# Interleaving the second half's attention with the first half's MLP in a one-core encoder layer

## The chip, the core and the metric

The kernel runs on one core of a Trainium2 chip. The core has a matrix engine (TensorE, PE in the profile; its weight loads are PEld), three elementwise engines (VectorE or DVE, ScalarE or ACT, GpSimd or POOL), and a queue engine (SyncE or SP) from which this kernel issues all its DMAs. TensorE results land in PSUM, which has eight banks of 512 float32 columns; everything else lies in SBUF, on 128 partitions. The engines run their own instruction streams in order and wait for one another by semaphores.

The metric is the device time of one execution in microseconds (us), the median of the runs shown.

## The reference, cut to what matters

One layer of a hybrid encoder: 1024 tokens, width 1024, float32.

```
mod = silu(c) @ w_ada + b_ada                 -> sh_a, sc_a, g_a, sh_m, sc_m, g_m
h    = rmsnorm(x) * (1+sc_a) + sh_a
proj = h @ w_in   -> q_lat (256), kv_lat (128), k_rope (32), ca_qkv (3 x 8 heads x 64)
q    = rmsnorm(q_lat) @ w_q_up                -> 8 heads x 96, QK-norm, rotary on 32
k, v = rmsnorm(kv_lat) @ w_kv_up (+ k_rope)   -> 8 heads x (96, 64), QK-norm, rotary
o_mla = softmax(q k / sqrt(96), keys of own and earlier 64-token chunks) @ v
cq, ck = rmsnorm(per head of ca_qkv)
o_ca  = softmax(cq ck / 8 + relative bias, own chunk and 8 chunks to the left) @ cv
x   = x + g_a * (concat(o_mla, o_ca) @ w_out)
h   = rmsnorm(x) * (1+sc_m) + sh_m
u   = causal_depthwise_conv3(h @ w_up) + b    -> gate, val (2816 each)
x   = x + g_m * ((silu(gate) * val) @ w_down)
```

Two facts decide what can overlap. The attention is causal by chunks, so the first 512 tokens need no key of the last 512. And everything after the attention is per token, except that the convolution of a token needs the up-projection of the two tokens before it.

## The kernel before

**Precision.** Every large float32 product is three products of a reduced-precision form: each operand is split into a high part and a low rest, and `gemm3` (L144) adds high x high, high x low and low x high, at L148, L149 and L150. The split of a weight tile is an ACT copy (`hi_of`, L75) and a subtraction on POOL or DVE (`lo_of`, L82). The softmax weights and V are split into two half-precision parts instead; there the product with V is a chain of 128 x 128 matmuls (L714).

**Stages.** The layer is done for all 1024 tokens, stage after stage:

1. Start (L191 to L326): eight tiles of x are loaded and normalised; for each of eight 128-channel slices d, a 1 MB piece of `w_ada` is reduced on DVE (L239, L241) to the shift and scale, the slice of x is transposed and modulated into the pages `hT` (L219 to L228), and the first block of the input projection is accumulated (`qk0`). Then come the rotary tables (L260), a chain of small DVE instructions.
2. Attention. A unit is four query tiles of 128 tokens of one head (`Unit`, L626). `scores` (L634) makes the scores of one query tile against all its keys in PSUM (L656), the row minimum (DVE L667, L671 or L675; the signs are turned), the exponential (ACT L681), the two half-precision parts (POOL L71 and DVE L701) and a DMA transpose of them (L703). `values` (L707) multiplies with V three tiles later (`DEPTH`), and after four tiles L721 and L722 combine the parts and the result goes to DRAM (`oT_d`). All units of the chunked heads come first, in both token halves, then all units of the latent heads (L812, L813).
3. Between the tiles of the attention, fillers (L771) put other products in: the V and q/k projections (`f_v`, `f_qk`), the latent block (`f_m`), the up-projections of the latent heads (`f_up`) and the output projection of the chunked heads (`f_oca`). `pace` (L803) releases fillers in proportion to the attention's matmul time, with the factor 1.9 beside the chunked heads and 0.5 beside the latent ones. A second list, `f_ada` (L417), reduces the other rows of `w_ada` on DVE.
4. Output projection of the latent heads, residual, second norm and the pages `h2` (L834 to L879), with nothing beside them; then the MLP's gate row (L896 to L908), again alone.
5. MLP (L910 to L963). For each of 44 channel tiles, `up_tile` loads and splits a 512 KB weight tile, makes 48 matmuls of 512 columns (24 for each token half), and applies the convolution (ACT L923, DVE L924, L925). For each pair of channel tiles `ff_tile` forms silu(gate) x val, splits it, and prepares a `w_down` tile. `down` takes two such results at a time and adds them into the residual rows x1 (DVE L951).

**What sets the order.** The program gives dependences and priorities only; a scheduler at build time orders each engine's instructions by a simulated clock, and gives a tile a buffer from the free ones of its tag. `tc.high_priority` lifts the attention's steps, `issue_after` (L161) holds a filler's matmuls behind the attention's recent ones. At run time each engine then takes its instructions in that fixed order. The buffers of the attention, of the transition and of the MLP are separate pools, opened and closed one after another; PSUM likewise (psA, psB, psC).

## Time and profile before

| | us |
|---|---|
| median of 3 runs | 1525.28 (1518.91 to 1527.24) |
| span of the profiled execution | 1526.0 |
| PE busy | 1338.1 |
| DVE busy | 824.4 |
| POOL busy | 664.7 |
| ACT busy | 487.4 |

No time of the profiled execution other than its span is given; the span lies among the three measured times, 0.7 us above their median, so what lies around it is too small to be told from the spread. DMA moved 142.90 MB, at 94 GB/s on average.

In the profile a matmul's duration contains its way through the array, and neighbours overlap: the 512-column matmuls of the MLP are listed at 390 ns, yet 442 of them start in 100 us, one in 226 ns. So a busy PE may still have room, and what TensorE must do is better counted as matmuls times their spacing.

### The profile page before, as it was taken

How to read it: one execution, taken by the hardware profiler on the slowest of the kernel's cores; microseconds unless marked ns; L12 is line 12 of the kernel's file. 1: busy time of each engine (PE TensorE's matmuls, PEld its weight loads, DVE VectorE, ACT ScalarE, POOL GpSimd, SP SyncE). 2: the span in 40 equal slices, each digit the busy share in tenths (PEclk: the TensorE clock that was granted, in tenths of full speed). 3: DMA queues.
4: the chain of work that ended last, by engine and by line, in shares of the span. 5: the costliest groups of instructions: out<-in, count | busy, mean ns of one | idle time of the engine just before them, and what ended most of it. 6: DMA issues, size and time to landing. Idle time of an engine off the chain costs nothing.

```text
span 1526.0 us, 19445 instructions
## 1 busy us (share of the span) xinstructions
PE 1338.1 (88%) x7100; PEld 1111.0 (73%) x7100; DVE 824.4 (54%) x1536; ACT 487.4 (32%) x919; POOL 664.7 (44%) x720
## 2 busy tenths in 40 slices
PE   3859989998767888858739999999999999999997
PEld 2749878987646666646528888888888888888885
DVE  6864786566768768843742433344334343434343
ACT  5443353343545545532413211212122121221200
POOL 5264463473799735435725231514314142341510
PEclk9979978989878899977859999999999999999998
DMA  7323657463613678787142110202112020110202
GB/s 270 133 67 73 138 119 142 121 131 94 122 40 70 150 143 174 165 181 247 56 138 69 56 55 28 70 30 67 42 42 69 15 83 28 56 56 28 70 1 110
DMA packets 202460, 142.90 MB, mean 94 GB/s; under 512 B 146294, under 2 KB 181242, under 8 KB 201340
## 3 DMA queue, kind: packets, MB, share of 16 engines
q1 hardware_dynamic: 202364, 141.66, 36.0%
q8 instruction: 56, 0.92, 0.3%
q14 instruction: 40, 0.33, 0.1%
HBM read 93.90 MB, written 13.11 MB: 70 GB/s over the span
## 4 chain that ended last, share of the span: by engine, by line
PE 63%; DMA 14%; DVE 10%; POOL 7%; issue 3%; ACT 2%; SPq 1%; POOLq 0%; DVEq 0%; ACTq 0%
PE up L148 10%; PE up L149 10%; PE up L150 10%; DMA aw<-w_ada 6%; PE dn L148 5%; PE dn L149 5%; PE dn L150 5%; DMA PTm<-hlm 4%; PE sc L656 2%; DVE adacc L241 2%; DVE aacc L428 1%; PE sm L656 1%; PE pvc L714 1%; POOL hlm L71 1%; DMA adaw<-w_ada 1%
## 5 line engine op out<-in xcount | busy, mean ns | idle before, releaser
L148 PE MATMUL up<-hT,wu_h 128*128 128x512 f32 x704 | 275.1, 391 | 0.0
L149 PE MATMUL up<-hT,wu_h 128*128 128x512 f32 x704 | 274.3, 390 | 0.0
L150 PE MATMUL up<-hT,wu_l 128*128 128x512 f32 x704 | 274.1, 389 | 0.0
L951 DVE TENSOR_TENSOR x<-x,dn 128x1024 f32<-128x1024 f32 x88 | 107.4, 1220 | 179.8 <-PE dn L150 179.8
L924 DVE SCALAR_TENSOR_TENSOR u<-up,pk,u 128x1023 f32<-128x1023 f32 x44 | 56.4, 1283 | 232.1 <-ACT u L923 232.1
L923 ACT ACTIVATE u<-up,pk 128x1024 f32<-128x1024 f32 x44 | 53.1, 1208 | 386.0 <-PE up L150 386.0
L149 PEld LDWEIGHTS up<-hT,wu_h 128*128 128x128 f32 x704 | 132.4, 188 | 28.0 <-issue 0.5
L148 PEld LDWEIGHTS up<-hT,wu_h 128*128 128x128 f32 x704 | 132.4, 188 | 27.9 <-issue 0.5
L82 POOL TENSOR_TENSOR wu_l<-wu_r,wu_h 128x1024 fp32r<-128x1024 f32 x44 | 105.7, 2402 | 107.9 <-PE up L149 60.1
L150 PEld LDWEIGHTS up<-hT,wu_l 128*128 128x128 f32 x704 | 132.4, 188 | 27.7 <-POOL wu_l L82 0.2
L77 POOL TENSOR_SCALAR wd<-wd_r 128x1024 fp32r<-128x1024 f32 x22 | 23.1, 1050 | 290.2 <-PE dn L150 289.1
L148 PE MATMUL dn<-wd,g 128*128 128x512 f32 x352 | 138.0, 392 | 5.0 <-ACT g L75 5.0
L149 PE MATMUL dn<-wd,g 128*128 128x512 f32 x352 | 137.9, 392 | 0.0
L150 PE MATMUL dn<-wd,g 128*128 128x512 f32 x352 | 137.4, 391 | 0.0
L71 POOL TENSOR_SCALAR hlm<-Pm,rim 128x512 f16<-128x512 f32 (+4 forms) x88 | 62.8, 717 | 69.1 <-DMA PTm<-hlm 46.6
L75 ACT ACTIVATE wu_h<-wu_r 128x1024 fp32r<-128x1024 f32 x44 | 46.5, 1057 | 141.1 <-DMA wu_r<-w_up 141.1
L938 POOL TENSOR_TENSOR wd_r<-wd_r,gmbc 128x1024 f32<-128x1024 f32 x22 | 52.6, 2392 | 80.6 <-DMA wd_r<-w_down 80.6
L701 DVE SCALAR_TENSOR_TENSOR hlm<-Pm,rim,hlm 128x512 f16<-128x512 f32 (+4 forms) x88 | 70.2, 801 | 31.7 <-POOL hlm L71 31.4
L148 PEld LDWEIGHTS dn<-wd,g 128*128 128x128 f32 x352 | 66.6, 189 | 19.4 <-issue 5.4
L71 POOL TENSOR_SCALAR hlc<-Pc,ric 128x640 f16<-128x640 f32 (+2 forms) x64 | 45.9, 719 | 78.5 <-DVE ric L684 38.9
L656 PE MATMUL sm<-mk,mq 96*128 96x512 f32 (+3 forms) x288 | 70.0, 375 | 9.8 <-ACT Pm L681 9.0
L656 PE MATMUL sc<-k,q 64*128 64x512 f32 (+3 forms) x288 | 71.2, 376 | 7.4 <-ACT Pc L681 4.9
(276 smaller groups left out, 3031.8 us busy)
## 6 DMA issues: line engine op xcount, KB each, us to landing
wu_r<-w_up SPq DMA_DIRECT2D x44, 512.0 KB, 3.6
aw<-w_ada SPq DMA_DIRECT2D x96, 128.0 KB, 2.2
wd_r<-w_down SPq DMA_DIRECT2D x22, 512.0 KB, 3.5
x<-x SPq DMA_DIRECT2D x16, 512.0 KB, 9.3
adaw<-w_ada_a SPq DMA_DIRECT2D x8, 1024.0 KB, 4.8
wq_r<-w_qk SPq DMA_DIRECT2D x32, 128.0 KB, 2.6
wor<-w_out SPq DMA_DIRECT2D x16, 256.0 KB, 3.0
cl<-oT_d SPq DMA_DIRECT2D x16, 256.0 KB, 3.3
```

The source lines that it names most:

```text
L71: pool.tensor_scalar(o, i, s, 1.0, op0=MUL, op1=MUL)
L75: act.activation(o, i, AF.Copy)
L82: (pool if eng == "p" else dve).tensor_tensor(o, i, f32(hi), op=SUB)
L148: pe.matmul(pt, sh, mh, start=(start and i == 0), stop=False)
L149: pe.matmul(pt, sh, ml, start=False, stop=False)
L150: pe.matmul(pt, sl, mh, start=False, stop=(stop and i == n - 1))
L656: last = pe.matmul(s[:, c:c + w], qpg[rs_, a, q], kpgs[kh][rs_, b, ko:ko + w], start=(a == 0 and b == 0), stop=(a == 1))
L701: dve.scalar_tensor_tensor(hl[:, w:2 * w], pp, ri[:], hl[:, :w], op0=MUL, op1=SUB)
L923: act.activation(u[:], pt[:], AF.Identity, scale=pk[:, cv + 2:cv + 3], bias=pk[:, cv + 3:cv + 4])
L924: dve.scalar_tensor_tensor(u[:, 1:], pt[:, :S - 1], pk[:, cv + 1:cv + 2], u[:, 1:], op0=MUL, op1=ADD)
L938: pool.tensor_tensor(raw[:], raw[:], gmbc[:], op=MUL)
L951: dve.tensor_tensor(x1[t][:], x1[t][:], pt[:], op=ADD)
```

## The change

The layer is cut into two halves of 512 tokens, h = 0 and h = 1.

- The start does only the first half: four tiles of x, pages `hT` of half 0, and the latent block instead of the first q/k block. The reduction of the first two `w_ada` pieces moves from DVE to TensorE, as products with one moving column.
- The first attention round runs all 16 heads of half 0. Its fillers are the projections of half 0 and of half 1 (`f_up`, `f_qk`, `f_v`, each now called once for each half, and so loading and splitting its weights twice), and `f_hT1` and `f_m1` for half 1. The factor of `pace` is 3.4.
- The finished q and k pages of half 1, the k pages of half 0 and all V tiles are written to DRAM (`keep_page`, `keep_v`) and read back by the units that use them (`get_page`, `load_v`).
- The second round runs all heads of half 1. Its fillers are the MLP's gate row, the whole output projection, residual and norm of half 0 (`f_op`, all eight heads' rows at once, no partial sums in DRAM), and the MLP of half 0. The factor is 4.0.
- Last come `f_op` and the MLP of half 1. The MLP therefore loads and splits all its weights twice. Each `up_tile` has 24 matmuls and a 512-column result; the convolution's two edge columns are carried from half 0 to half 1 (`cvt`, `cvc`).
- All SBUF tiles come from one pool with a fixed number of slots for each role (`BUFS`), all PSUM tiles from another (`PB`). The result tiles of `up_tile` and `down` shrink from two buffers of 1024 columns each to two shared buffers of 512.

```diff
+    BUFS = {"H": 10, "X": 4, "w": 8, "raw": 2, "g": 3, "T": 8, "pg": 5, "HL": 3, "PT": 3, "R": 8,
+            "V": 2, "bias": 2, "tg": 1}
+    PB = {"S": 2, "mm": 2, "T": 1, "pv": 1}
...
+    def load_cols(name, src, ncol, kk, he="a", le="p", ssw=None):
...
+        for k0 in range(0, ND, kk):
+            raw = sb("raw", [P, kk, ncol], f"{name}r{k0}")
+            sp.dma_start(raw[:], src[:, k0:k0 + kk, :])
...
+            hi = sb("w", [P, kk, ncol], f"{name}h{k0}", F32R)
+            lo = sb("w", [P, kk, ncol], f"{name}l{k0}", F32R)
+            hi_of(he, hi[:], raw[:])
+            lo_of(le, lo[:], raw[:], hi[:])
...
+    for d in range(ND):
+        if d + 2 < ND:
+            load_ada(d + 2)
+        pt = psum("mm", f"p_ada{d}")
+        for i in range(2):
+            for k in range(ND):
+                pe.matmul(pt[:, i:i + 1], wada[d, i][:, k], cs[:, k:k + 1], start=(k == 0), stop=(k == ND - 1))
...
+        hT[d, 0] = mod_transpose(lambda j: xs[j][:, d * P:(d + 1) * P], d, 0, 0, ("T", "pv")[d % 2],
+                                 "H", "a", "v" if d % 2 else "p")
...
+    def keep_page(key, pg, rows):
+        d = dram.tile([P, 2, 512], F32, name="pgd_" + "_".join(map(str, key)))
+        sp.dma_start(d[:rows], f32(pg[:rows]))
+        pg_d[key] = d
+
+    def get_page(key, rows):
+        pg = sb("pg", [P, 2, 512], "pgl_" + "_".join(map(str, key)), F32R)
+        sp.dma_start(f32(pg[:rows]), pg_d[key][:rows])
+        return pg
...
+    def f_qk(p, h):
+        w = load_cols(f"wq{p}{h}_", I["w_qk"][p], 256, 4)
+        qn = sb("T", [P, 4, 256], f"qn{p}_{h}")
...
+        if h == 0:
+            qns[p] = qn
+        else:
+            for kind, c, gain in (("q", 0, None), ("k", P, gk_ca[:])):
+                pg = qk_page(lambda j: qn[:, j, c:c + P], f"{kind}{p}_1", P, gain)
+                keep_page(("c", p, kind, 1), pg, P)
+                yield 440
...
+        def load_v(u, grp, hd):
+            u.v = sb("V", [P, 8, P], f"vl{u.nm}_{u.g}", F16)
+            for h in range(u.g + 1):
+                sp.dma_start(u.v[:, 4 * h:4 * h + 4], v_d[grp, h][:, :, hd])
...
-                if n <= 640:
-                    pr = at.tile([P, 640], F32, name=f"P{nm}", tag="P", bufs=P_BUFS)
-                else:
-                    pr = pgtile([P, 1024], F32, f"P{nm}")
+                pr = sb("R", [P, 512], f"P{nm}") if n <= 512 else sb("T", [P, 1024], f"P{nm}")
...
+            else:
+                u.pages = (get_page(("m", gr, hh, "q", 1), QK), [get_page(("m", gr, hh, "k", i), QK) for i in range(2)])
...
+    def f_op(h, otag, xtag, ntag, h2tags):
+        oh = []
+        for t in range(4):
+            x1[h, t] = sb(xtag, [P, D], f"x1_{h}{t}")
+            sp.dma_start(x1[h, t][:], I["x"][(4 * h + t) * P:(4 * h + t + 1) * P, :])
+            lo = sb(otag, [P, ND, P], f"ol{h}{t}", F32R)
+            hi = sb(otag, [P, ND, P], f"oh{h}{t}", F32R)
+            for k in range(ND):
+                sp.dma_start(f32(lo[:, k]), oT_d[h][k][:, t * P:(t + 1) * P])
+            hi_of("a", hi[:], f32(lo[:]))
+            lo_of("p", lo[:], f32(lo[:]), hi[:])
...
+        def up_tile(ch):
+            raw = sb("raw", [P, ND, P], f"wur{h}_{ch}")
+            sp.dma_start(raw[:], I["w_up"][ch])
+            hi = sb("w", [P, ND, P], f"wuh{h}_{ch}", F32R)
+            lo = sb("w", [P, ND, P], f"wul{h}_{ch}", F32R)
+            hi_of("a", hi[:], raw[:])
+            lo_of("p", lo[:], raw[:], hi[:])
+            pt = psum("mm", f"up{h}_{ch}")
+            yield from gemm3_f(pt[:], [(hi[:, k], lo[:, k], h2[k, h][:, 0], h2[k, h][:, 1]) for k in range(ND)])
...
+    attend([mla_unit(0, hh, 0) for hh in range(4)] + [ca_unit(p, 0, o) for p in range(2) for o in range(2)]
+           + [mla_unit(1, hh, 0) for hh in range(4)] + [ca_unit(p, 0, o) for p in range(2, 4) for o in range(2)], R_G0)
...
+    fillers += [("gm", f_ada((5,))), ("op0", f_op(0, "H", "X", "T", ["H"] * 8)), ("mlp0", f_mlp(0))]
+    attend([ca_unit(p, 1, o) for p in range(4) for o in range(2)]
+           + [mla_unit(gr, hh, 1) for gr in range(2) for hh in range(4)], R_G1)
...
+    with tc.high_priority(offset=3000):
+        for _ in f_op(1, "T", "pg", "T", ["T"] * 4 + ["H"] * 4):
+            pass
+    for g in mlp0:
+        for _ in g:
+            pass
+    for _ in f_mlp(1):
+        pass
```

965 lines of the change are left out of this document (445 added, 520 removed).

## The prediction

> **What bounds the kernel now.** I read first the slices of the span, then busy time by stage, then the groups of instructions for durations, then the waits.
>
> ```profile
> PE   3859989998767888858739999999999999999997
> PEclk9979978989878899977859999999999999999998
> ```
>
> From slice 22 on (the MLP) PE is full and its granted clock is full. Ahead of it neither is. By stage (columns: window, length, then busy us and count of each engine, clock, DMA share, GB/s):
>
> ```profile
> 0.00:72.00 72.00, 41.77 (x251) 36.05 (x252) 53.69 (x117) 34.97 (x59) 28.57 (x42) 0.96 0.59 210
> 72.00:130.00 58.00, 40.27 (x293) 36.03 (x292) 37.63 (x123) 26.80 (x71) 29.29 (x38) 0.82 0.26 66
> 130.00:400.00 270.00, 251.70 (x1754) 220.32 (x1753) 176.38 (x508) 110.13 (x299) 134.05 (x203) 0.91 0.57 122
> 400.00:500.00 100.00, 72.50 (x390) 57.68 (x388) 76.04 (x200) 55.62 (x137) 93.23 (x172) 0.82 0.31 65
> 500.00:680.00 180.00, 142.83 (x986) 113.37 (x985) 132.43 (x311) 85.05 (x176) 91.70 (x112) 0.92 0.76 159
> 680.00:797.00 117.00, 69.93 (x276) 52.98 (x276) 60.73 (x59) 32.66 (x49) 58.85 (x48) 0.71 0.47 152
> 797.00:1526.00 729.00, 719.09 (x3162) 594.53 (x3160) 287.48 (x220) 142.12 (x131) 228.99 (x109) 0.99 0.17 52
> ```
>
> The MLP is bound by PE. At 400 to 500, where the latent heads are projected up, POOL is 93% busy; from 500 to 680 nothing is full; from 680 to 797 there is little to do beside the transition. For what TensorE must do I use spacings:
>
> ```profile
> 900.00:1000.00 100.00, 100.00 (x442) 82.79 (x442) 42.65 (x32) 22.83 (x22) 36.54 (x17) 1.00 0.18 56
> ```
> ```profile
> 240.18 0.28 PE L148 MATMUL ipv<-wv_s,hT 128*128 128x256 f32 x1
> 240.30 0.28 PE L149 MATMUL ipv<-wv_s,hT 128*128 128x256 f32 x1
> ...
> 620.79 1.39 PE L714 MATMUL pvm<-PTm,vt 128*128 128x128 f16 x22
> ```
>
> That is 100/442 = 0.226 us at 512 columns and 0.12 at 256, so 0.014 + 0.000414 per column between; 0.056 for a product with V (22 in 1.39, the last listed at 0.22); four transposes in 0.60 (the last 0.27) are 0.11 each. From 72 to 797 the old order holds 576 q/k (69 us), 384 V (46), 192 latent (36), up-projection (27), scores (92), products with V (59), output projection 384 (87), transposes (31) and some 7 of the rest: 454 us of PE work in 725. So 271 us are idle, slow or switching, and only this the change can win. The MLP's 3168 matmuls (716 us) stay.
>
> ```profile
> L923 ACT ACTIVATE u<-up,pk 128x1024 f32<-128x1024 f32 x44 | 53.1, 1208 | 386.0 <-PE up L150 386.0
> L82 POOL TENSOR_TENSOR wu_l<-wu_r,wu_h 128x1024 fp32r<-128x1024 f32 x44 | 105.7, 2402 | 107.9 <-PE up L149 60.1
> L75 ACT ACTIVATE wu_h<-wu_r 128x1024 fp32r<-128x1024 f32 x44 | 46.5, 1057 | 141.1 <-DMA wu_r<-w_up 141.1
> L71 POOL TENSOR_SCALAR hlm<-Pm,rim 128x512 f16<-128x512 f32 (+4 forms) x88 | 62.8, 717 | 69.1 <-DMA PTm<-hlm 46.6
> ```
> ```profile
> L931 ACT ACT_TABLE_LOAD x1 | 1.3, 1283 | 0.9 <-DVE u L925 0.9
> ```
>
> The sum is made against the profiled span of 1526.0 us; the median is 0.7 less, which I neglect.
>
> **Start, to the last page of x.** Before, it ended at 72, the pieces of `w_ada` following one another at 6.3 us (44 us between the first and eighth product). Now a piece costs PE 32 one-column matmuls (16 calls in two passes each, as the old row shows them; four in 0.50 us give 0.11 each, 3.5 us), one page's transposes (0.4) and 12 latent matmuls (2.2): 6.1 us, no faster than the loads' 4.8 us landing. With 2 MB less of x ahead I put the first at 13 us: 13 + 8 x 6.3 = **63** (58 to 72). DVE loses its 39 us here; the rotary tables (about 25 us) take that place.
>
> **Stage A, first-half attention with all projections.** PE work: q/k 92, V 46, up-projections 27, latent of half 1 18, scores of half 0 28, products with V 320 x 0.056 = 18, 248 transposes 27, the rest 5: 261. POOL: low parts of weights 78 (now 16 x 2.40 for q/k alone, since each block is loaded twice), up-projections 16 x 4.1 = 66 (one power call fewer per tile), q/k norms 16 x 2.7 = 44, softmax parts 34, latent rows 27, pages and norm 10: 259. DVE: softmax 97, 48 pages 34, up-projections 44, `w_ada` rows 32, V, norms and combinations 35, the rest 20: 262. ACT: exponentials 46, pages 32, up-projections 37, high parts 34, the rest 91: 240. So four engines are loaded nearly alike, and what the old stages reached with such a mix decides. There PE work plus busy DVE, ACT and POOL came to (201 + 176 + 110 + 134)/270 = 2.30, (48 + 76 + 56 + 93)/100 = 2.73 and (117 + 132 + 85 + 92)/180 = 2.37 engines; together 2.40. 1022 us of work is 374 us at 2.73 and 426 at 2.40. I take **400**, between, because one stage now has all kinds of work at hand, as no old one had. The 36 page stores (16 MB) and the V stores lie on DMA and SP: 64 transposes at 1.24 us and some 250 other issues at 0.3 to 0.5 are 180 of SP's 400 us.
>
> **Stage B, second-half attention with the first half's MLP.** PE: scores 64, products with V 736 x 0.056 = 41, output projection 192 x 0.226 = 43, MLP 1584 x 0.226 = 358, transposes and gate row 6: 512. DVE: softmax and combinations 176, convolution 88 x 0.74 = 65, additions of `down` 88 x 0.68 = 60, silu product and low part 35, the rest 37: 373. POOL: 44 x 2.40 = 106, `w_down` 22 x 4.8 = 105, softmax parts 60, output projection 40: 311. ACT: exponentials 68, high parts 46 + 23, results 42, silu 26, the rest 35, and up to 44 table loads (below) 56: 296. PE is the largest. As bounds: 512/0.98 = 522, the MLP's own share, and 512/0.82 = 622, by the 2.40 engines again (1492/2.40). What PE lost at 130 to 400 was 18 us idle and 51 of clock and of switching between narrow and wide matmuls; the same 64 tiles are switched to here, so I take some 50, and 18 for the gate row and output projection that must come ahead of the first MLP weight: **580**. A tile comes only every 9 us, and its values are used three tiles later, so a softmax chain of about 10 us and a landing of 3.3 us are covered, also where SP has to wait with a weight load (SP waited 175.8 us for the low part of `w_up` to free its buffer) and the transposes queue behind it. DMA moves about 60 MB, at 52 GB/s per 0.17 some 196 us, and 736 transposed blocks some 140 us: 58% of the stage, below the 0.76 of 500 to 680.
>
> **Stage C, the rest.** Output projection 43, pages 4, MLP 358. PE idle: the pacing has 105 x 4.0 = 421 us to give and 406 of fillers, so the last two tiles run bare, 10; then combination 1.4, store 2.5, eight loads issued at 0.46, landing 3.3, split 1.06 + 2.40: 14; norm 5; pages one at a time in the single transpose bank, 8 x 2.2 less the first weight tile's 5.4: 12. At the end silu chain, addition and store: 9. Sum **456** (440 to 480). The halved result tiles of `down` leave 1.36 us of matmuls for an addition of about 0.7 and its handoffs; alone that holds, so I cost it at nothing here.
>
> 63 + 400 + 580 + 456 = **1499 us**.
>
> **ACT's tables.** The old profile has three table loads of 1283 ns, since every exponential comes before every silu. Now 22 silus of half 0 lie among 64 exponentials: at most 44 loads, 56 us of ACT, in the sum as load and not on the path. [...]
>
> **The rivals.**
>
> Weights late in stage B (slower): while four of the eight weight slots hold `w_down` tiles, two pairs are left for `w_up`, so the next split starts when the last tile but one is done. It takes 1.06 + 2.40 = 3.5 us against 5.4 of matmuls, 1.9 to spare. If an exponential with its sum (1.1), a table load (1.28) and a softmax part (0.72) stand ahead, 3.1, each of 66 tiles is 1.2 us late: 79 us, **1578**. It turns the sign (1533) from 0.5 us per tile. For it: POOL and ACT take orders fixed beforehand. Against: in the old MLP they idled 100 and 141 us ahead of these splits.
>
> Table loads on the path: 44 x 1.283 = 56 us behind exponentials that PE waits for, **1555**. Against: three tiles of slack.
>
> Stage A stalls on its slots: eight "T" slots hold four token tiles per up-projection, the V tile, q/k rows and `w_ada`'s sum; at 2.3 engines, as at 130 to 400, A is 444: **1543**.
>
> It does all it says: A at 2.73 engines, B at 535, C at 445: 63 + 374 + 535 + 445 = **1417**.
>
> No change: the idle time moves from the old transition into A and B, **1525**.
>
> **How the numbers follow.** Forecast 0.33; all it says 0.18; weights late 0.25; slots in A 0.09; table loads 0.07; no change 0.08. Faster by over 0.5% (about what this kernel's measurement can tell) 0.51, same 0.08, slower 0.41. The forecast's own range, from A's two ends, is 1473 to 1518 (1525, cut where it would count as no change); with the bounds of A and B and the cases of both signs, 1425 to 1605.
>
> **What would show it.** Start right: last page of x's first half near 63. A: second-half scores from 463, no engine over 80%. B: `up` matmuls among scores, clock 0.95 or more, PE work 88% of 580. C: one gap of PE under 45 us, then 226 ns spacing. Weights late: PE idle ahead of `up` put down to POOL's low parts or ACT. Wrong altogether if A takes over 450, by a filler that waits for a slot, or if the additions of `down`, on half the buffer, hold PE.

## The result, and the profile after

The changed kernel takes **1683.7 us** (median of 4, 1680.5 to 1692.4) against 1523.5 for the old one measured beside it: a ratio of **1.107** (95% interval 1.104 to 1.110). It is slower by a tenth, where 1499 us was forecast, and outside the range. The profiled execution spans 1680.0 us, 154 more than the old one's 1526.0.

The busy tenths and the granted clock in forty slices, the same two rows of the page as before the change:

```profile
PE   7955798778994597988989999999796999999998
PEclk9676898887796597999999999999897999999999
```

From slice 17 to 28 PE is now nearly full, and it dips again in slices 29 and 31. But slices 1 to 16 are as ragged as before. By stage (columns: window, length, then busy us and count of PE, weight loads, DVE, ACT and POOL, granted clock, DMA share, GB/s), with the whole of stage A in the last row:

```profile
0.00:84.70 84.70, 74.89 (x384) 72.77 (x384) 25.03 (x93) 23.64 (x36) 20.89 (x27) 0.82 0.50 184
84.70:143.70 59.00, 25.78 (x113) 19.64 (x113) 23.35 (x46) 24.97 (x66) 42.51 (x77) 0.65 0.26 83
143.70:465.20 321.50, 264.09 (x1695) 229.87 (x1695) 201.22 (x500) 145.73 (x346) 175.84 (x206) 0.85 0.61 156
465.20:560.60 95.40, 58.28 (x392) 50.55 (x391) 38.70 (x71) 35.55 (x64) 55.31 (x67) 0.77 0.62 184
560.60:659.40 98.80, 77.88 (x358) 61.62 (x358) 58.82 (x108) 29.03 (x46) 49.03 (x36) 0.78 0.60 173
659.40:1208.30 548.90, 497.64 (x2574) 395.94 (x2574) 341.85 (x590) 227.43 (x352) 277.86 (x167) 0.95 0.57 140
1208.30:1296.00 87.70, 66.47 (x266) 51.06 (x266) 26.15 (x28) 24.41 (x30) 52.45 (x32) 0.84 0.29 91
1296.00:1680.00 384.00, 361.72 (x1545) 288.44 (x1543) 216.44 (x266) 120.43 (x150) 195.98 (x82) 0.99 0.28 88
...
84.70:560.60 475.90, 348.15 (x2197) 300.07 (x2197) 263.27 (x615) 206.25 (x476) 273.65 (x350) 0.81 0.57 153
```

The cuts are events: 84.7 is the last latent product of the start, 143.7 the first score, 465.2 the last score of the first half, 560.6 the first of the second, 659.4 the first `up` product, 1208.3 the last `down` product of the first half. The second half's last product with V is at 1204.3; below, stage B ends there and stage C is the rest. The stretch from 1208.3 to the second half's first `up` product at 1274.6 is called the join. The start varies from run to run: the nine other kernels below that keep it as it is ended it at 89.4 to 93.8 us.

PE's work below is counted as in the prediction, by products times their full-rate spacing. "Idle" is time with no product under way, "low rate" what is left: products at a lower clock, and switching between forms (in the old kernel's trace, at a clock of 1.00, the 256-column product at 248.83, right behind one with V, starts 0.20 us ahead of the next, where within a run of them it is 0.12).

| stage | forecast | measured | PE work | idle | low rate |
|---|---|---|---|---|---|
| start | 63 | 84.7 | 50 | 10 | 25 |
| A | 400 | 475.9 | 262 | 128 | 86 |
| B | 580 | 643.7 | 507 | 72 | 65 |
| C | 456 | 475.7 | 409 | 43 | 24 |
| old kernel, 72 to 797 | | 725 | 459 | 148 | 118 |

Of the 10 us idle in the start, 9 lie ahead of its first product. Where do the 154 us come from? Take the start off, and the MLP's 358 us of PE work that now lies in the middle. The rest, up to the first `up` product of the second half (1274.6), is 1274.6 - 84.7 - 358 = 832 us; the old kernel did the same between 72 and 797, in 725. So: start +13, projections and attention **+107**, the MLP, with its first half counted at the full rate (358 + 405 against 729), +34.

The groups that answer to those shown of the old kernel:

```profile
L834 ACT ACTIVATE u<-up,pk 128x512 f32<-128x512 f32 x88 | 67.3, 766 | 72.5 <-PE up L145 72.5
L80 POOL TENSOR_TENSOR wul<-wur,wuh 128x1024 fp32r<-128x1024 f32 x88 | 213.6, 2427 | 194.0 <-ACT wuh L73 191.9
L73 ACT ACTIVATE wuh<-wur 128x1024 fp32r<-128x1024 f32 x88 | 92.9, 1056 | 163.2 <-PE dn L144 96.2
L69 POOL TENSOR_SCALAR hlm<-Pm,rim 128x512 f16<-128x512 f32 (+4 forms) x88 | 60.3, 689 | 84.3 <-DMA PTm<-hlm 25.4
```
```profile
L676 ACT ACT_TABLE_LOAD x14 | 18.0, 1283 | 48.0 <-DVE rim L678 38.2 <-DVE ric L678 3.9 <-DVE mm L673 3.2
L846 ACT ACT_TABLE_LOAD x14 | 18.0, 1283 | 10.2 <-DVE u L838 10.1
```

Their durations are the old ones (2427 against 2402 ns, 1056 against 1057, 689 against 717). There are twice as many weight splits, and 29 table loads (the 28 shown and one at the start) where there were three. So these instructions are not slower, and the time has to be looked for in their order and in what they wait for.

### The profile page after: what moved, and what is told of

It reads as the page before. It is cut to its first block, busy times and chain, and to the rows that moved or that the text cites. A ratio compares the mean times of both kernels' runs of the same rounds, so it can differ in the third digit from the quotient of the medians.

```text
span 1680.0 us, 20674 instructions
## 1 busy us (share of the span) xinstructions
PE 1426.8 (85%) x7320; PEld 1169.9 (70%) x7320; DVE 931.6 (55%) x1698; ACT 631.2 (38%) x1088; POOL 869.9 (52%) x692
## 4 chain that ended last, share of the span: by engine, by line
PE 39%; DVE 14%; DMA 9%; ACT 6%; POOL 5%; issue 5%; SPq 1%; ACTq 0%; POOLq 0%; DVEq 0%
PE up L144 6%; PE up L143 6%; PE up L145 5%; PE dn L143 4%; PE dn L144 3%; PE dn L145 3%; DMA PTm<-hlm 2%; PE sm L654 2%; ACT wuh L73 2%; PE sc L654 2%; DVE hlc L686 2%; DVE u L837 2%; DVE u L847 2%; DVE u L838 2%; POOL wul L80 2%
## 5 line engine op out<-in xcount | busy, mean ns | idle before, releaser
L80 POOL TENSOR_TENSOR wul<-wur,wuh 128x1024 fp32r<-128x1024 f32 x88 | 213.6, 2427 | 194.0 <-ACT wuh L73 191.9
L145 PE MATMUL up<-hT,wul 128*128 128x512 f32 x704 | 278.2, 395 | 5.9 <-POOL wul L80 5.9
L143 PE MATMUL up<-hT,wuh 128*128 128x512 f32 x704 | 277.7, 398 | 5.5 <-DVE u L838 3.4
L144 PE MATMUL up<-hT,wuh 128*128 128x512 f32 x704 | 279.1, 396 | 2.2 <-POOL hT L211 2.0
L867 DVE TENSOR_TENSOR x<-x,dn 128x512 f32<-128x512 f32 x176 | 119.9, 683 | 91.2 <-PE dn L145 90.4
L143 PE MATMUL dn<-wdh,g 128*128 128x512 f32 x352 | 148.7, 422 | 19.1 <-DVE x L867 12.4
L143 PEld LDWEIGHTS up<-hT,wuh 128*128 128x128 f32 x704 | 134.2, 191 | 35.9 <-ACT wdh L73 3.8
L145 PEld LDWEIGHTS up<-hT,wul 128*128 128x128 f32 x704 | 134.1, 190 | 35.5 <-POOL wul L80 7.6
L144 PEld LDWEIGHTS up<-hT,wuh 128*128 128x128 f32 x704 | 134.3, 191 | 32.2 <-POOL hT L211 2.9
L73 ACT ACTIVATE wuh<-wur 128x1024 fp32r<-128x1024 f32 x88 | 92.9, 1056 | 163.2 <-PE dn L144 96.2
L144 PE MATMUL dn<-wdl,g 128*128 128x512 f32 x352 | 140.9, 400 | 0.0
L145 PE MATMUL dn<-wdh,g 128*128 128x512 f32 x352 | 140.5, 400 | 0.0
L80 POOL TENSOR_TENSOR wdl<-wdr,wdh 128x1024 fp32r<-128x1024 f32 x44 | 108.2, 2459 | 38.4 <-ACT wdh L73 37.4
L143 PEld LDWEIGHTS dn<-wdh,g 128*128 128x128 f32 x352 | 68.2, 194 | 47.8 <-DVE x L867 23.6
L145 PEld LDWEIGHTS dn<-wdh,g 128*128 128x128 f32 x352 | 68.2, 194 | 15.7
```

Of the source, the lines that this page charges most:

```text
L73: act.activation(o, i, AF.Copy)
L80: (pool if eng == "p" else dve).tensor_tensor(o, i, f32(hi), op=SUB)
L143: pe.matmul(pt, sh, mh, start=(start and i == 0), stop=False)
L144: pe.matmul(pt, sh, ml, start=False, stop=False)
L145: pe.matmul(pt, sl, mh, start=False, stop=(stop and i == n - 1))
L867: dve.tensor_tensor(x1[h, t][:, c], x1[h, t][:, c], pt[:], op=ADD)
```

## The experiments

Four theories to begin with. *Slots*: fillers wait for single banks and few buffers (the transposes' one PSUM bank, two raw weight slots, `down`'s half-size results). *Order*: leftover projections, the gate row and the output projection run with too little beside them. *Tables*: ACT's reloads stand on the path. *One-column products*: they slow the start. All runs are against the old kernel timed in the same session; gains below are differences of ratios times 1523 us, and by the intervals each is good to some 7 us.

| run | edit on | median us | ratio to old [interval] |
|---|---|---|---|
| changed kernel | | 1683.7 | 1.107 [1.104, 1.110] |
| e1 pace of A | changed | 1693.7 | 1.112 [1.108, 1.117] |
| e2 `down` in one tile, second half | changed | 1680.9 | 1.102 [1.098, 1.106] |
| e3 start's sum on DVE | changed | 1677.5 | 1.100 [1.097, 1.104] |
| e4 no silu in the first half | changed | 1671.0 | 1.097 [1.093, 1.101] |
| e5 PSUM banks in A | changed | 1656.0 | 1.083 [1.080, 1.086] |
| e6 A without `w_ada` loads | changed | 1674.6 | 1.096 [1.092, 1.100] |
| e7 gate row beside projection | changed | 1673.3 | 1.096 [1.092, 1.101] |
| e8 output in one transfer | changed | 1687.6 | 1.103 [1.100, 1.106] |
| e9 `w_down` raw in page slot | e2 | 1669.5 | 1.097 [1.093, 1.101] |
| e10 q/k heads first | changed | 1716.5 | 1.129 [1.125, 1.132] |
| e11 banks and pace | e5 | 1663.7 | 1.093 [1.089, 1.096] |
| e12 e3+e5+e7+e9 | changed | 1609.2 | 1.056 [1.053, 1.059] |
| e13 second split left out | e12 | 1594.6 | 1.046 [1.043, 1.049] |
| e14 page stores left out | e12 | 1600.6 | 1.050 [1.047, 1.053] |
| e15 second attention run bare | e12 | 1700.1 | 1.115 [1.112, 1.118] |
| e16 `w_down` raw in T slot, first half | e12 | 1583.2 | 1.038 [1.035, 1.041] |
| e17 no drain after A | changed | 1684.6 | 1.106 [1.101, 1.111] |
| e18 e16 + e8 + list order | e16 | 1571.8 | 1.032 [1.028, 1.036] |

### e1: pace

```
-R_G0, R_G1 = 3.4, 4.0
+R_G0, R_G1 = 4.4, 4.0
```


> The first half's attention is given more filler work per tile (4.4 in place of 3.4), so that no projection is left over when it ends; nothing else changes. After: 84 to 560 us, of which 470 to 560 is leftover work with only 36 us of TensorE work in it. Theory 'order' (the leftover runs bare): the last 90 us shrink and the stage goes from 476 to 430 to 445 us, the time from 1684 to 1640 to 1655. Theory 'slots' (the fillers stall on single banks and few buffers wherever they stand): the attention is stretched by what the tail loses, the stage stays at 465 to 480, the time at 1672 to 1688.

It came out 8 us slower, outside both ranges and nearer the rival; the two intervals still touch, so no gain is what is shown. From the start's last product to the second half's first score took 488 us in place of 476: the attention was stretched (last score at 535) by more than the tail lost. More filler per tile did not make the fillers faster.

### e2 and e9: down's result tile, then the raw slots

```
-                    pt = psum("mm", f"dn{h}{t}{n}_{len(fs)}")      # two tiles of 512, two additions
+                    pt = psum("S", f"dn{h}_{t}_{len(fs)}", 1024)   # h == 1: one tile, one addition
...
-            raw = sb("raw", [P, D], f"wdr{h}_{j}")                 # e9, on top of e2
+            raw = sb("raw" if h == 0 else "pg", [P, D], f"wdr{h}_{j}")
```


> Only in the second half's MLP, the result of the down projection goes back to one tile of 1024 columns in the score banks (then idle) with one addition of 1024. Theory 'halved buffers': TensorE's waits for the additions (8.3 us of matmuls and 16.6 of weight loads in the trace of after) go, the MLP from 1296 on takes 360 to 368 in place of 384 us, the time falls from 1684 to 1662 to 1670. Rival: the additions only show up as the last of several events, the MLP stays within 5 us, 1679 to 1688.

> e2 (down's result in one 1024-column tile in the second half's MLP) and, in the same MLP, the raw tile of w_down in one of the page slots, idle by then, in place of the raw slots, so that w_up has both raw slots to itself. In e2 the waits for down's additions went, and 23.8 us of waits for the low part of w_up on POOL came in their place, once per group of two tiles, behind a landing of 3.5 us and 4.25 us of POOL work on w_down. Theory 'raw slots': these go too; the first up product of that MLP to the end, 401 us in after and 397 in e2, takes 375 to 385, and the time is 1655 to 1668. Rival 'POOL's order': the split of w_up still stands behind w_down's 4.8 us on POOL, 392 to 400 us, 1674 to 1684.

PE's groups in the second half's MLP (1300 to 1675), of the changed kernel and then of e2, by line: busy and mean, then the idle time ahead of them and what ended it:

```profile
L143 PE MATMUL dn<-wdh,g 128*128 128x512 f32 x176 | 71.9, 409 | 14.2 <-DVE x L867 8.3 <-DVE u L838 3.6 <-DVE u L840 1.8
L143 PEld LDWEIGHTS dn<-wdh,g 128*128 128x128 f32 x176 | 33.0, 187 | 33.0 <-DVE x L867 16.6 <-issue 9.6 <-ACT g L73 0.9
```
```profile
L145 PE MATMUL up<-hT,wul 128*128 128x512 f32 x336 | 132.7, 395 | 10.0 <-POOL wul L80 10.0
L143 PE MATMUL dn<-wdh,g 128*128 128x512 f32 x176 | 69.7, 396 | 4.1 <-ACT g L73 4.1
L145 PEld LDWEIGHTS up<-hT,wul 128*128 128x128 f32 x336 | 63.6, 189 | 27.0 <-POOL wul L80 13.8
```

The waits for `x` (the additions of `down`) are gone in e2, as the theory said, and the stretch from the first `up` product to the last product of the kernel fell only from 401 to 397 us: waits for the low part of `w_up` of about the same size (24 us for 25, products and weight loads added) stand in their place. The rival's figures came true: the first wait was real, and it covered a second. e9 gives `w_up` both raw slots. The waits for POOL go from these groups, and the stretch takes 388 us, 13 less than in the changed kernel (375 to 385 were expected, by the rival 392 to 400). The time of e2 alone can't be told from no change (the intervals overlap); that of e9 can, by 15 us.

### e3: the start

```
-                pe.matmul(pt[:, i:i + 1], wada[d, i][:, k], cs[:, k:k + 1], ...)   # 16 per piece
+                dve.scalar_tensor_tensor(acc[:], wada[d, i][:, k], cs[:, k:k + 1], acc[:], op0=MUL, op1=ADD)
+            pe.matmul(pt[:, i:i + 1], acc[:], ones[:, 0:1], start=True, stop=True)
...
-        if d == 1:
+        if d == ND - 1:
             rope_tables()
```


> The start's reduction of w_ada goes back to VectorE (16 multiply-adds of 128 columns per piece, two one-column products left per piece in place of 16); the rotary tables come after the loop, as before the change. Theory 'one-column products slow the start' (27 of its 84 us, at 0.213 us each, and the clock with them): the start ends at 62 to 72, the granted clock in it is over 0.9, the time 1662 to 1675. Rival 'the loads and VectorE set the start': VectorE has 128 such steps of some 0.3 us, 38 us, beside the pages; the start stays at 78 to 88 and the later tables add up to 10; 1680 to 1695.

The start's groups, of the changed kernel and of e3:

```profile
L305 PE MATMUL p_ada<-cs,adaw 128*128 128x1 f32 x256 | 42.8, 296 | 0.1
```
```profile
L307 DVE SCALAR_TENSOR_TENSOR adacc<-adaw,cs,adacc 128x128 f32<-128x128 f32 x112 | 38.3, 405 | 0.0
L143 PE MATMUL lat<-wm_h,hT 128*128 128x416 f32 x32 | 15.8, 495 | 13.3 <-ACT hT L205 13.3
L308 PE MATMUL p_ada<-ones,adacc 128*128 128x1 f32 x32 | 6.4, 294 | 8.9 <-DVE adacc L307 8.8
```

PE is free of 43 us, and the start ends at 81.7 us; in the other three kernels of that session, whose start is unchanged, it ended at 89.6 to 92.4. So some 8 us of the start, 10 of the time, not 20: PE now waits for VectorE's sum and for the pages `hT` that need it, and the granted clock stayed at 0.82, where over 0.9 was expected. Half right each.

### e4: tables

```
-            act.activation(ug[:], ug[:], AF.Silu)
+            if h == 1:
+                act.activation(ug[:], ug[:], AF.Silu)
```


> The silu of the first half's MLP is left out (the half's gate is then linear), so that ACT has no table to change while the second half's attention runs; the 22 activations themselves (26 us of ACT) go with it. Theory 'table loads on the path': stage B goes from 648 to 590 to 615 us, the time to 1625 to 1650. Theory 'slack covers them' (as forecast): B stays at 635 to 648, the time at 1668 to 1684.

Stage B fell from 643.7 to 635.4 us, the time by 14. The 36 us of loads, and the activations with them, are covered but for that, as the rival had it; *tables* falls as the main cause.

### e5: PSUM banks, and e11: banks with pace

```
-    PB = {"S": 2, "mm": 2, "T": 1, "pv": 1}                  # S of 1024 columns
+    PB = {"S": 2, "mm": 3, "T": 2, "pv": 1}                  # S of 512, until A has ended
...
+    psA.__exit__(None, None, None)
+    PB.update(S=2, mm=2, T=1, pv=1)
```


> Until the first half's attention has ended, score tiles are 512 columns wide (that half needs no more), and the two PSUM banks this frees go to the fillers: two banks for transposes in place of one, three for results in place of two. From then on the banks are as in after. Theory 'PSUM slots' (A is held by the single transpose bank and two result banks): the idle and low-clock time of 84 to 560 falls, the stage from 476 to 420 to 450 us, and its tail from 470 on most of all; time 1625 to 1660. Rival 'weights' (A follows the chain of loads through the two raw slots and the low parts on POOL): the stage stays at 465 to 480, only the pages at its end gain some 5 to 10 us; time 1670 to 1685.

> e5 (two transpose banks and three result banks in the first half's attention) and the pace of e1 (4.4 in place of 3.4, nothing left over when that attention ends). With the old banks the pace alone gained nothing. Theory 'PSUM slots held the pace': now the fillers keep up, start's end to the second half's first score falls from 433 (e5) to 400 to 418 us, time 1638 to 1645. Rival 'the engines' chains hold it': 428 to 440 us, time 1650 to 1662.

In the changed kernel the leftover's pages go through one bank, one behind the other. Its timeline (PE, ACT and DVE; start, duration, instruction, and in brackets the idle time before it and what ended that):

```profile
540.11 1.09 PE L354 MATMUL mq_ps<-ident,qt 128*96 128x128 f32 x4 [1.56 <-DVE mk L361]
541.24 0.59 ACT L357 ACTIVATE mq<-mq_ps 96x512 fp32r<-96x512 f32 x1 [1.96 <-PE mq_ps L354]
541.86 0.69 DVE L358 TENSOR_TENSOR mq<-mq_ps,mq 96x512 fp32r<-96x512 f32 x1 [1.81 <-ACT mq L357]
542.61 1.09 PE L354 MATMUL mk_ps<-ident,kt 128*96 128x128 f32 x4 [1.41 <-DVE mq L358]
...
545.25 1.09 PE L354 MATMUL mq_ps<-ident,qt 128*96 128x128 f32 x4 [1.55 <-DVE mk L361]
```

That is a page each 2.57 us, three engines in turn, each waiting for the one before. The waits of PE ahead of the pages' transposes over all of stage A, changed kernel and then e5:

```profile
L354 PE MATMUL mq_ps<-ident,qt 128*96 128x128 f32 x64 | 14.6, 338 | 29.3 <-POOL qt L391 22.4 <-DVE mk L361 4.7 <-DVE k L361 1.7
L354 PE MATMUL mk_ps<-ident,kt 128*96 128x128 f32 x64 | 13.0, 341 | 12.4 <-DVE mq L358 10.5 <-DVE bias L715 1.9
L354 PE MATMUL k_ps<-ident,qn 128*128 128x128 f32 x32 | 6.5, 338 | 7.7 <-DVE q L358 7.7
```
```profile
L355 PE MATMUL mq_ps<-ident,qt 128*96 128x128 f32 x64 | 14.8, 341 | 21.1 <-POOL qt L392 18.6 <-DVE mq L359 2.4
L355 PE MATMUL mk_ps<-ident,kt 128*96 128x128 f32 x64 | 14.4, 336 | 16.3 <-POOL kt L564 16.2
L355 PE MATMUL k_ps<-ident,qn 128*128 128x128 f32 x32 | 6.7, 313 | 1.3 <-DVE mk L362 1.3
```

Stage A of e5 as one window:

```profile
98.80:531.50 432.70, 328.14 (x2197) 290.39 (x2196) 258.15 (x615) 205.28 (x477) 280.14 (x350) 0.84 0.63 167
```

The waits for DVE to empty the bank (`mk`, `mq`, `q`, `k`) fall from 25 to 4 us; POOL's rotary parts of the token tiles (`qt`, `kt`) are next. Stage A takes 433 us, 43 less, with the same work of every engine: 23 of the 43 were idle and the rest low rate. The time falls by 36: the largest single cause found, in the range that *slots* gave. The start, where the edit also moves two latent results into the banks of tag `mm`, ended later, at 98.8, so by the second half's first score the gain is 29 us. The tail, which *slots* had most of all in mind, gave 13 of the 43; 25 came from beside the attention. The waits in the rows above account for 11 only, and no run parts the second transpose bank from the third result bank. With the faster pace added (e11) the stage is 443 and the time 14 us worse again, a little beyond the rival's figures: pace was not held by these banks.

### e6: the loads of w_ada's rows

```
-                w = sb("raw", [P, D], f"aw{m}_{k}")
-                sp.dma_start(w[:], I["w_ada"][k * P:(k + 1) * P, m * D:(m + 1) * D])
+                if m == 5:
+                    w = sb("raw", [P, D], f"aw{m}_{k}")
+                    sp.dma_start(w[:], I["w_ada"][k * P:(k + 1) * P, m * D:(m + 1) * D])
+                elif k:
+                    w = acc
```


> The 24 loads of w_ada's rows for the gate, shift and scale in the first half's attention are left out (512 KB each, through the two raw slots that the projection weights share); VectorE's multiply-adds stay, on their own sum, so the modulation is wrong and the amount of VectorE work is not. Theory 'weights' (chain of loads through the raw slots; aw<-w_ada is 4.1% of the chain, each landing in 4 to 5 us): the stage 84 to 560 falls by 30 to 60 us, the time to 1625 to 1655. Rival 'PSUM slots': the loads wait behind other things anyway, the stage falls by under 10, time 1672 to 1685.

`w_ada`'s rows are not loaded here, except for the MLP's gate. From the first score of the first half to that of the second: 409 us in place of 417, as the rival had it. The time fell by 16 us, so the loads cost something, but not the 30 to 60 that their place in the chain (`aw<-w_ada` 4.1% of it) suggested. What a chain names is not what its removal gives.

### e7: the gate row

```
-    fillers += [("gm", f_ada((5,))), ("op0", ...), ("mlp0", f_mlp(0))]
+    side[0] = f_ada((5,)); EVERY[0] = 2500
+    fillers += [("op0", ...), ("gm", side[0]), ("mlp0", f_mlp(0))]
```


> In the second half's attention the row of w_ada for the MLP's gate is made beside the first half's output projection, a step for each 2.5 us of it, in place of ahead of it; the rest of that row then follows, and the MLP after it. In after, the output projection starts 33 us after the second half's first score, and the first product of the MLP 99 us after it. Theory 'order': both come 20 to 30 us earlier, the time falls to 1655 to 1668. Rival 'weights': the gate row's eight loads and the output projection's weights share the two raw slots, so what one gains the other loses; the MLP starts 90 to 99 us after the first score, the time is 1676 to 1690.

The first `up` product came 82 us after the second half's first score instead of 99, and the time fell by 16: *order*, a little less than it asked.

### e8: one transfer for the attention's output

```
-            for k in range(ND):
-                sp.dma_start(f32(lo[:, k]), oT_d[h][k][:, t * P:(t + 1) * P])
+            sp.dma_start(f32(lo[:]), oT_t[h][:, :, t * P:(t + 1) * P].rearrange("k p t -> p k t"))
```


> The attention's output comes back in one transfer per token tile in place of eight (as in the old kernel), so SP issues 8 in place of 64; the layout in DRAM is one tensor per half. Theory 'SP issue on the path' (eight issues of 0.43 us stand between the last store and each first split of the join, and 14 us of them ahead of the weights in round two): the join, 88 us from the last down product to full rate, falls by 6 to 12, and the MLP's start in round two by 5 to 10; time 1664 to 1675. Rival: the weights' splits set the join (wor 3.6, ACT 1.07, POOL 2.4 for each), it falls by under 4; time 1678 to 1686.

The intervals overlap; no gain shown, as the rival had it.

### e10: q/k heads first

```
-    fillers += [("up00", ...), ("x1", ...), ("qk00", ...), ("v00", ...), ("up10", ...), ...
+    fillers += [("qk00", ...), ("v00", ...), ("x1", ...), ("qk10", ...), ("up00", ...), ("qk20", ...), ...
-    attend([mla_unit(0, hh, 0) ...] + [ca_unit(p, 0, o) ...] + ...
+    attend([ca_unit(p, 0, o) ...] + [mla_unit(0, hh, 0) ...] + ...
```


> The first half's attention begins with the four heads of q/k and V (as the old kernel did) in place of the four latent heads, and its fillers with the first q/k and V blocks. In after, TensorE has 16 us of work in the 59 from the last product of the start to the first score, and POOL, with the latent rows and their up-projection, is busy 42.5 of them. Theory 'order': the first score comes 25 to 35 us after the start's last product, the stage shrinks by 15 to 30, time 1655 to 1670. Rival 'slots': what is gained at the front is lost at the first latent head, the second half's first score comes within 8 us of where it did, time 1676 to 1690.

A miss for both: the first score came 41 us after the start in place of 59, and then everything was later, 1716 us. Stage A took 500. PE waited 21 us for the transposed softmax (`PTm`) and 21 for the latent heads' token tiles, where the changed kernel has 8 and 7. The order that was there is better than the old one at this place.

### e12: the four gains together

> e3, e5, e7 and e9 in one: VectorE reduces w_ada in the start, wide banks for the first half's fillers, the gate row beside the output projection, down's result in one tile and w_down's raw tile in a page slot in the last MLP. If their gains stand in different places they add up: 10 + 34 + 16 + 15, against the same old kernel 1600 to 1615. If they are one cause under several names (a chain that moves on to the next slot), 1625 to 1645. That it beats the old kernel's 1525 neither theory says.

1609.2 us. The single gains (10 + 36 + 16 + 15 = 77) and the measured one (77) agree, more closely than their errors promise: they are separate places, not one chain under several names. It leaves 86 us over the old kernel: start 81, A 441, B 622, C 463.

### e13 and e14: what the halves cost twice

```
-            lo = sb("w", [P, kk, ncol], f"{name}l{k0}", F32R)          # e13, for the second half
-            lo_of(le, lo[:], raw[:], hi[:])
+            lo = hi
...
-        d = dram.tile([P, 2, 512], F32, name="pgd_" + ...)             # e14
-        sp.dma_start(d[:rows], f32(pg[:rows]))
+        # all but the first page and V tile of each kind read that one
```


> On e12 (1609 us). The weight blocks that the second half's projections load again are not split again: their low part is left out and the high part stands in for it, so the products' number is the same, some 45 us of POOL's low parts in the stage go and the second half's projections are less exact. Theory 'every weight block split twice': the stage from the start's end to the second half's first score, 441 us in e12, falls to 400 to 420, time 1572 to 1592. Rival 'softmax chains and pages': POOL has room, the stage falls by under 10, time 1598 to 1610.

> On e12. All but two of the page stores and two of the V stores are left out; later loads read those four, so the attention's pages and V are wrong, and the number and size of loads is the same. Theory 'the way through DRAM': 34 stores on SP and up to 500 KB each on DMA go, with what queues behind them; the stage of 441 us falls by 15 to 30, time 1578 to 1595. Rival: SP and DMA have room there (DMA share 0.69), the stores are not waited for, time 1602 to 1612.

e13: stage A 425 in place of 441, time less by 16: between the two theories. e14: A 438, B 616 in place of 622, time less by 10: nearer the rival. Both are prices of the split into halves, and both are small beside the rest.

### e15: the interleave alone undone

```
-R_G0, R_G1 = 3.4, 4.0
+R_G0, R_G1 = 3.4, 0.0        # and f_op(1, ...) after the first half's MLP
```


> On e12, with the interleave of the second half's attention undone: that attention runs with no filler beside it, then the first half's output projection and MLP, then the second half's. Theory 'the interleave pays': 64 tiles bare take 180 to 260 us, then 70 to the first up product and 360 for the MLP; from the second half's first score to the last down product of the first half, 622 us in e12, 640 to 690; time 1640 to 1720. Rival 'what it hides it gives back in the MLP': 590 to 625 us there, time 1590 to 1625.

The second half's attention with nothing beside it, by window, and three of the largest waits from 560 to 787 (total, times, longest):

```profile
519.40:787.90 268.50, 199.32 (x1143) 159.54 (x1142) 171.25 (x435) 71.72 (x143) 72.41 (x88) 0.64 0.83 177
```
```profile
POOL hlm L69 <- DMA PTm<-hlm: 76.6, 31, 9.2
POOL hlc L69 <- DVE ric L683: 51.7, 17, 7.9
PE pvm L703 <- DMA PTm<-hlm: 30.0, 18, 5.1
```

268 us for 110 us of PE work; the softmax's transposing DMA is the longest wait, and the DMA engines are 83% busy. Then come 464 us for gate row, projection and MLP up to the second half's output projection: 732 against 628 in e12, more than either theory gave. The time is **some 90 us worse**, within the range of 'the interleave pays'. So, with the halves and their buffers as they are, the interleave pays. The kernel is slower through what the halves and their buffers cost, not through the interleaving itself.

### e16: raw slots in the first half's MLP

```
-            raw = sb("raw" if h == 0 else "pg", [P, D], f"wdr{h}_{j}")
+            raw = sb("T" if h == 0 else "pg", [P, D], f"wdr{h}_{j}")
```


> On e12, with the raw tile of w_down in the first half's MLP in one of the eight slots of tag T in place of the two raw slots (as e9 did it for the second half with a page slot). Theory 'raw slots': the stretch from the first up product to the end of the second half's attention, 545 us in e12 with 446 us of TensorE work in it, falls to 515 to 532, time 1580 to 1598. Rival 'the chain of the softmax and its fixed order on the engines': under 6 us, time 1603 to 1613.

From the first `up` product to the attention's end, e12 and then e16:

```profile
599.30:1144.00 544.70, 493.71 (x2551) 390.79 (x2552) 339.65 (x586) 226.36 (x350) 280.01 (x168) 0.95 0.56 140
```
```profile
600.40:1128.10 527.70, 490.61 (x2558) 388.64 (x2558) 318.24 (x584) 230.22 (x355) 284.50 (x170) 0.96 0.59 146
```

17 us shorter, with the same work; the time 28 us less, both in the ranges that *raw slots* gave. The waits of PE beside the first half's MLP show how the slots reached it (600 to 1045 of e12, then 601 to 1053 of e16; total, times, longest):

```profile
PE sm L658 <- ACT Pm L680: 16.6, 9, 4.5
PE sc L658 <- ACT Pc L680: 8.5, 6, 3.8
```
```profile
PE sm L658 <- ACT Pm L680: 1.8, 3, 0.8
PE sc L658 <- ACT Pc L680: 1.5, 3, 0.6
```

These are scores that wait for an exponential to leave their bank, 25 us in e12 and 3 in e16. In the same stretches ACT stood 21 us ahead of its weight splits until `wur` had landed, and in e16 no such wait is left. That the exponentials stood behind those splits in ACT's order is the likely link; no run shows it one by one.

### e17: no drain, and e18: the best version

```
-    while fill_step() is not None:                              # e17; up11 ahead of the last q/k and V, R_G1 = 4.5
-        pass
...
-        u.need = [f"qk{p}0"] if g == 0 else []
+        u.need = [f"qk{p}{g}"]
```


> On the changed kernel itself: the second half's attention starts at once when the first's ends, and the projections left over by then (two q/k blocks and one V block of the second half) become the first fillers beside it; the latent heads' second up-projection moves ahead of them, into the first half's attention, and the second half's pace is 4.5 in place of 4.0 so that the longer list is used up. Theory 'order' (the leftover's 95 us with 36 us of TensorE work ran bare): the gap from the first half's last score to the second half's first, 95 us, falls under 20, stage B grows by 40 to 55 for what it takes over, time 1640 to 1660. Rival 'chains': the leftover takes as long beside the attention as bare, the first up product comes within 10 us of 659, time 1675 to 1690.

> e16 (1583 us), with e8 (one transfer per token tile for the attention's output) and the latent heads' second up-projection ahead of the last q/k and V blocks, so that the leftover is of long products and not of sixteen pages. If the leftover's pages and the issues cost what the chains show (16 pages of 2.5 us each behind the one before, 24 issues of 0.43 us at the join): 1558 to 1574. If only the end of the list changes its name: 1577 to 1590.

e17 gained nothing. The second half's first score came only 67 us after the first half's last, and the first `up` product at 679 in place of 659. The second half's first key pages were not asked for until 526.9: in that gap SP waited 24 us for DVE ahead of the page stores of the moved up-projection, and the loads stand behind them in SP's queue. What was taken from the gap came back as a later MLP, so 'order' falls for the leftover too, with the reservation that the attention did not start at once, as it was meant to. The time is in the rival's range, but its sign is not: the first `up` product came 20 us from 659, not within 10.

e18, with the raw slots, e8 and the up-projection's sixteen pages ahead of the last q/k and V, takes 1571.8 us, in the first of the two ranges: 115 less than the changed kernel, still 3.2% (2.8 to 3.6) above the old one. Over e16 it gains 10 us, and the two intervals still touch. Its stages are 80, 429, 603 and 462.

## Why the prediction was wrong, point by point

Of the 181 us that the forecast was short of the profiled span, 22 came in the start, 76 in A, 64 in B and 20 in C.

**Start, 63.** Measured 84.7. The failed term is the piece's price on PE, 6.1 us, which took the full rate for granted. The 256 one-column products took 42.8 us, 0.167 each, 5.35 per piece in place of 3.5, and the latent products 28 us for 18 of work. But 0.167 is a mean of two rates. Two groups of them (start, duration of the group), and a window inside each, where the clock is the third figure from the end:

```profile
34.59 1.84 PE L305 MATMUL p_ada<-cs,adaw 128*128 128x1 f32 x16
47.29 5.97 PE L305 MATMUL p_ada<-cs,adaw 128*128 128x1 f32 x28
```
```profile
34.60:36.40 1.80, 1.80 (x18) 1.80 (x17) 0.00 (x0) 0.84 (x1) 0.51 (x1) 1.00 0.89 349
47.30:53.30 6.00, 6.00 (x30) 6.00 (x30) 0.69 (x1) 1.45 (x2) 0.00 (x0) 0.50 0.29 90
```

At a clock of 1.00 they follow one another at the 0.11 us of the sum, at 0.50 at 0.21 (ahead of 31 us they are 0.21 apart too, although the windows there show 1.00). From its first product at 8.9 us PE was idle for 1 us only, so PE set the start. A part, 8 us, is shown (e3), where the waits for VectorE's sum and the pages take the products' place.

**Stage A, 400: the step that failed.** The load was right: PE 262 us of work (forecast 261), DVE 263 (262), POOL 274 (259), ACT 206 (240). "What the old stages reached with such a mix decides" was the mistake, and with it "I take 400, between". The sum, 1005 us in 476, is 2.11 engines at once, below the lowest stage it was taken from (2.30). How many engines ran at once depended on the banks that the work passes through (2.11 with the changed kernel's, 2.32 with those of e5), and the sum had no term for banks and slots, although it charged stage C for "pages one at a time in the single transpose bank". The old attention has the same banks (one for transposes, two for results), but it put 54 such tiles through the transpose bank in 725 us, and the new stage 62 in 476. With two, and three result banks, the same 1005 us take 433, which is 2.32 engines, and so 36 us of the time (e5). Whether the old kernel would gain by such banks too was not run. Argued from the old figures, and shown by no run: the averaging skipped the old kernel's poor ends; over all of 72 to 797 it reached (459 + 483 + 310 + 407) / 725 = 2.29, which would have given 446. The new stage has such ends too, 59 us at the front with 16 of PE work and 95 at the back with 47. The second split and the stores through DRAM, which were in the sum as load, are 16 and 10 us of time (e13, e14, on e12). The text's own sign, A over 450 "by a filler that waits for a slot", is what happened; the rival named the SBUF slots of tag T; shown are the PSUM banks.

**Stage B, 580.** Measured 643.7, with 507 us of PE work (forecast 512). The forecast allowed 68 us of loss; it was 137. Shown of it: the gate row ahead of the projection, 16 us (e7), two raw slots for four weight streams, 17 us of the stage (e16). So the failed step is "I take some 50, and 18". The tile's slack did not wholly cover the softmax chain, as the prediction had argued: scores waiting for exponentials were PE's largest wait beside the first half's MLP, 25 us in e12 and 3 once the raw slots were eased (e16). Still the cover is real: bare, the same attention takes 268 us, interleaved it adds some 164 to the 464 of the rest (e15). Some half of the 69 us beyond the allowance is not traced to a cause.

**Stage C, 456.** Measured 475.7. Idle is 43 us where some 50 were in the sum, but 18 of it lie between the MLP's products, where none was to be, and 24 at a low rate were not counted. What failed is "the halved result tiles of `down` ... I cost it at nothing". The additions held PE, as the last sentence of the prediction allowed, and behind them the raw slots did: 13 us together in the stretch (e9).

**Tables, in the sum as load only.** Right: 28 loads rather than 44, and leaving out their cause moves stage B by 8 us and the time by 14, silu's own activations included. The trace shows each load at 1283 ns and 36 us in all, off the path but for those few.

**Rivals.** "Stage A stalls on its slots" was the right one, at 44 us above the forecast's stage where 76 came. "Weights late in stage B" was right that weights bind, but by the raw slots and not by the eight weight slots, and with 17 us shown where it had 79. The mistake of the whole: each rival was given a chance as if only one could happen, and the likeliest case was one in which none did. They were separate places, most of them happened in part, and e12 shows that such prices add (77 and 77).

What stays open: e18 is 48 us above the old kernel and 73 above the forecast, 17 of that in the start, 29 in A, 23 in B and 6 in C. A at 429 us has 87 us of idle PE, and no run here tells how much of it falls to the POOL chain of the token tiles that e5 uncovered. A third raw slot in A, or more slots of tag T, were not tried.

## What to carry to other kernels

Adding up engine work gives a stage's load, not its length: before an old stage's concurrency is used for a new one, list each bank and slot that a step of the new one holds, and for how long (one bank passed from PE to ACT to DVE and back made a page each 2.57 us, whatever else was idle). Where an edit shrinks several buffers at once, charge each place and add the charges; mending one shows the next (e2, e9, e16). And an interleave that pays (90 us here) can still lose, if what it takes to collect the cover (halves, second splits, smaller buffers) costs more.

## What was unexpected in the hardware

In the changed kernel's join PE's products ran at about half the rate behind a gap in its work (start, duration, instruction, idle before it):

```profile
1211.53 0.40 PE L144 MATMUL op<-wol,oh 128*128 128x512 f32 x1
1216.67 0.80 PE L143 MATMUL op<-woh,oh 128*128 128x512 f32 x1 [4.75 <-ACT oh L73]
1217.26 0.63 PE L144 MATMUL op<-wol,oh 128*128 128x512 f32 x1
1217.69 0.63 PE L145 MATMUL op<-woh,ol 128*128 128x512 f32 x1
```

After 4.75 us without work, the starts are 0.43 us apart where the same product takes 0.23, for 5.1 us (until 1222.4); the granted clock is 0.50 from 1212.3, 0.4 us after the last product ahead of the gap, to 1222.4, 5.7 us after the restart. The old kernel's trace has the like at its end: after 5.02 us without work the `down` products from 1498.8 on start 0.43 us apart, and the granted clock, 0.50 from 1496.2, some 3 us into that gap, is 1.00 again from 1503 on. Stage A has a granted clock of 0.81, and 86 us at a low rate beside 128 idle. Whether the one follows from the other there, no run shows: none took the gaps away alone.

In the start the clock fell with no gap at all. From 38.1 to 58.5 us PE's products follow one another and the granted clock is 0.50. The clock fell three times there (at 38.1, 68.8 and 75.6 us), each time in or just behind a run of one-column products, and rose again (at 58.5, 72.2 and 82.4) behind latent products of 416 columns. Why it fell there, no run shows: e3, which takes most of the one-column products out, has waits in their place and the same mean clock of 0.82.
